# Part of a load goes over 15 DMA engines, so that the sixteenth carries 8 KB less

## The chip, the cores and the metric

One core of a Trainium2 chip. The metric is the device time of one execution in microseconds (us). The kernel before takes 120.12 us (median of three runs, 120.01 to 120.28).

## The reference

```python
x, y: (1024, 4096) float32
z = x * y
out = 0.5 * z * (1 + tanh(sqrt(2 / pi) * (z + 0.044715 * z ** 3)))
```

## The kernel before

Each of 128 partitions owns eight rows, 32,768 contiguous elements (128 KB) of x, y and the output. SP issues all transfers. x stays in SBUF whole, y goes through a ring of half that size; DVE multiplies in place, ACT applies the activation in place, and two stores take the halves out.

```python
X_LOADS = [(0, 16384), (16384, 32768)]
Y_LOADS = [(0, 16384, 0), (16384, 24576, 0), (24576, 31488, 8192), (31488, 32768, 15104)]
STORES  = [(0, 16384), (16384, 32768)]
...
def load_x(i):
    a, b = X_LOADS[i]
    return nc.sync.dma_start(out=xs[:, a:b], in_=x_r[:, a:b]).then_inc(sem_x[i], 16)
...
_hoist(nc, [load_x(0).ins, load_y(0).ins])        # issued first of all
load_x(1)
for i in range(1, len(Y_LOADS)):
    nc.sync.wait_ge(sem_mul, -(-(Y_LOADS[i][1] - Y_RING) // STEP))   # ring space is free
    load_y(i)
... # DVE waits for sem_x >= 16 and sem_y >= 16, multiplies; ACT follows
for i, (a, b) in enumerate(STORES):
    if i == 0:
        nc.sync.wait_ge(sem_y[-2], 16)            # no store before the third y load has landed
    nc.sync.wait_ge(sem_act, done[b])
    nc.sync.dma_start(out=out_r[:, a:b], in_=xs[:, a:b]).then_inc(sem_o[i], 16)
```

The queue of each DMA engine is thus: x first half, y first half, x second half, three pieces of y, two stores. The packet records of the trace before agree: eight packets an engine for each (65,536 bytes three times, then 32,768, 27,648, 5,120, and 65,536 twice), with an increment of 4 bytes after every eight.

Of the kernel before, what the change touches and what calls it, by code (L numbers as in the profile page):

```python
# [1 line left out]

# [4 lines left out]


F32 = mybir.dt.float32
GELU = mybir.ActivationFunctionType.Gelu_apprx_tanh  # L10


X_LOADS = [(0, 16384), (16384, 32768)]

Y_LOADS = [
    (0, 16384, 0),
    (16384, 24576, 0),
    (24576, 31488, 8192),
    (31488, 32768, 15104),
]  # L20
STEP = 4096
STORES = [(0, 16384), (16384, 32768)]
Y_RING = 16384


def _hoist(nc, issued):

    here = nc.cur_bb.bb.instructions
    first = nc.main_func.blocks[0].instructions
    for ins in issued:  # L30
        del here[next(k for k, i in enumerate(here) if i is ins or i.name == ins.name)]
    engine = issued[0].engine
    at = next(
        k
        for k, i in enumerate(first)
        if i.engine == engine and type(i).__name__ == "InstDrain"
    )
    first[at:at] = issued


@with_exitstack
def kernel(
    ctx: ExitStack,
    tc: tile.TileContext,
    x: bass.AP,
    y: bass.AP,
    out: bass.AP,
):
    nc = tc.nc
    P = nc.NUM_PARTITIONS  # L50

    x_r = x.flatten_outer_dims().rearrange("(p a) c -> p (a c)", p=P)
    y_r = y.flatten_outer_dims().rearrange("(p a) c -> p (a c)", p=P)
    out_r = out.flatten_outer_dims().rearrange("(p a) c -> p (a c)", p=P)
    total_f = x_r.shape[1]


    tc.close()
    tc.compile()  # L59

    xs = nc.alloc_sbuf_tensor("xs", [P, total_f], F32).ap()
    ys = nc.alloc_sbuf_tensor("ys", [P, Y_RING], F32).ap()
    sem_x = [nc.alloc_semaphore(f"sem_x{i}") for i in range(len(X_LOADS))]
    sem_y = [nc.alloc_semaphore(f"sem_y{i}") for i in range(len(Y_LOADS))]
    sem_mul = nc.alloc_semaphore("sem_mul")
    sem_act = nc.alloc_semaphore("sem_act")
    sem_o = [nc.alloc_semaphore(f"sem_o{i}") for i in range(len(STORES))]

    def load_x(i):
        a, b = X_LOADS[i]  # L70
        return nc.sync.dma_start(out=xs[:, a:b], in_=x_r[:, a:b]).then_inc(sem_x[i], 16)  # L71

    def load_y(i):
        a, b, r = Y_LOADS[i]
        return nc.sync.dma_start(
            out=ys[:, r : r + b - a], in_=y_r[:, a:b]
        ).then_inc(sem_y[i], 16)

    _hoist(nc, [load_x(0).ins, load_y(0).ins])
    load_x(1)  # L80
    for i in range(1, len(Y_LOADS)):
        nc.sync.wait_ge(sem_mul, -(-(Y_LOADS[i][1] - Y_RING) // STEP))
        load_y(i)

    n = 0
    done = {}
    for i, (a, b, r) in enumerate(Y_LOADS):
        for j, (xa, xb) in enumerate(X_LOADS):
            if xa <= a < xb:
                nc.vector.wait_ge(sem_x[j], 16)  # L90
        nc.vector.wait_ge(sem_y[i], 16)  # L91
        for c in range(a, b, STEP):
            w = min(STEP, b - c)
            nc.vector.tensor_mul(  # L94
                out=xs[:, c : c + w],
                in0=xs[:, c : c + w],
                in1=ys[:, r + c - a : r + c - a + w],
            ).then_inc(sem_mul, 1)
            n += 1
            done[c + w] = n  # L100
            nc.scalar.wait_ge(sem_mul, n)
            nc.scalar.activation(  # L102
                out=xs[:, c : c + w], in_=xs[:, c : c + w], func=GELU
            ).then_inc(sem_act, 1)

    for i, (a, b) in enumerate(STORES):
        if i == 0:
            nc.sync.wait_ge(sem_y[-2], 16)
        nc.sync.wait_ge(sem_act, done[b])
        nc.sync.dma_start(out=out_r[:, a:b], in_=xs[:, a:b]).then_inc(sem_o[i], 16)  # L110
    for i in range(len(STORES) - 1):
        nc.sync.wait_ge(sem_o[i], 16)
    nums = sorted(s.num for s in [*sem_x, *sem_y, *sem_o[:-1], sem_mul, sem_act])
    assert nums == list(range(nums[0], nums[-1] + 1))
    nc.sync.sem_clear(range(nums[0], nums[-1] + 1))
    nc.sync.wait_ge(sem_o[-1], 16).then_inc(sem_o[-1], -16)


# [1 line left out]
_INS = ['x', 'y']  # L120
_OUTS = [((1024, 4096), 'float32')]


# [23 lines left out]
```

## Time and profile before

| | before |
|---|---|
| time, median of 3 | 120.12 us |
| span of the trace | 118.7 us |
| DVE busy / ACT busy | 34.9 / 30.2 us |
| share of 16 DMA engines' time that packets fill | 98.6% |
| last landing of second x load / second y load / third y load / last store | 60.43 / 70.14 / 78.52 / 118.69 us |

The page is read from its DMA rows: compute is under a third busy, the DMA engines are full nearly everywhere. The landings are the times at which the trace sees each engine's increment of a transfer's semaphore. The lines themselves stand in the prediction.

### The profile page before, as it was taken

To read this page: it belongs to the slowest core of one execution; us is meant where nothing else is said; L and a number is where in the kernel's file an instruction comes from. 1 tells how busy PE (TensorE), PEld (TensorE's weight loads), DVE (VectorE), ACT (ScalarE), POOL (GpSimd) and SP (SyncE) were. 2 spreads that over 40 slices of the span, in tenths; PEclk is the share of its full clock that TensorE was granted. 3 is DMA by queue.
4 is the path that set the end of the run, shared out by engine and by line. 5 is a ranking of instruction groups with operands and counts; after the bars stand their busy time and mean duration, and the time that the engine had idled before them with its cause. 6 is when DMAs were issued, how large, how long until landed. Compare 5 with 4: busy or idle time off the path is not lost.

```text
span 118.7 us, 73 instructions
## 1 busy us (share of the span) xinstructions
DVE 34.9 (29%) x9; ACT 30.2 (25%) x10; POOL 0.2 (0%) x4
## 2 busy tenths in 40 slices
DVE  0000000000000199999700039999950000000000
ACT  3000000000000006797790000878995000000000
POOL 0000000000000000000000000000000000000000
DMA  9899888998899888988898989998889888988895
GB/s 353 353 420 640 353 353 353 662 397 353 353 552 508 353 353 375 684 353 353 353 497 386 453 375 447 447 574 353 353 353 707 353 353 353 707 353 353 353 486 221
DMA packets 1152, 50.33 MB, mean 424 GB/s; under 512 B 128, under 2 KB 128, under 8 KB 256
## 3 DMA queue, kind: packets, MB, share of 16 engines
q1 hardware_dynamic: 1152, 50.33, 98.6%
HBM read 33.55 MB, written 16.78 MB: 424 GB/s over the span
## 4 chain that ended last, share of the span: by engine, by line
DMA 51%; DVE 18%; ACT 6%; issue 0%; SPq 0%; DVEq 0%
DMA ys<-in_y_dram 51%; DVE xs L94 18%; ACT xs L102 6%; SPq L71 0%; DVEq L91 0%
## 5 line engine op out<-in xcount | busy, mean ns | idle before, releaser
L94 DVE TENSOR_TENSOR xs<-xs,ys 128x4096 f32<-128x4096 f32 (+2 forms) x9 | 34.9, 3946 | 52.8 <-DMA ys<-in_y_dram 52.8
L102 ACT ACTIVATE xs<-xs 128x4096 f32<-128x4096 f32 (+2 forms) x9 | 28.9, 3235 | 58.5 <-DVE xs L94 58.5
L102 ACT ACT_TABLE_LOAD x1 | 1.3, 1283 | 1.9 <-PEq L59 1.9
L131 POOL MEMSET const-bfloat16-1.0<- 128x1 bf16 x1 | 0.1, 102 | 0.0
L131 POOL MEMSET const-uint8-127<- 128x1 uint8 x1 | 0.1, 102 | 0.0
L131 POOL MEMSET const-float32-0.0<- 128x1 f32 x1 | 0.1, 99 | 0.2 <-issue 0.2
L131 POOL MEMSET const-float32-1.0<- 128x1 f32 x1 | 0.1, 99 | 0.0
## 6 DMA issues: line engine op xcount, KB each, us to landing
ys<-in_y_dram SPq DMA_DIRECT2D x1, 4096.0 KB, 20.2
ys<-in_y_dram SPq DMA_DIRECT2D x1, 3456.0 KB, 19.9
ys<-in_y_dram SPq DMA_DIRECT2D x1, 640.0 KB, 21.0
xs<-in_x_dram SPq DMA_DIRECT2D x2, 40.1
out_dram<-xs SPq DMA_DIRECT2D x2, 24.5
ys<-in_y_dram SPq DMA_DIRECT2D x1, 40.6
```

Source lines behind the costliest of these rows:

```text
L94: nc.vector.tensor_mul(out=xs[:, c : c + w], in0=xs[:, c : c + w], in1=ys[:, r + c - a : r + c - a + w],).then_inc(sem_mul, 1)
L102: nc.scalar.activation(out=xs[:, c : c + w], in_=xs[:, c : c + w], func=GELU).then_inc(sem_act, 1)
L131: nc = _bacc.Bacc("TRN2", target_bir_lowering=False, num_devices=1)
```

## The change

The intent is to take work off the DMA engine that is thought to end last. A transfer over 120 partitions is spread over 15 engines, and one over 8 partitions over 8; if 256 of the 16,384 columns go that way, one engine carries 8 rows of 1 KB less, and eight carry one more each. The trace before shows 16 landings for each of its transfers over 128 partitions and no other shape. The records don't number the engines: "the sixteenth" is the name of the one that carries less here, and "the first eight" are those with nine rows of 1 KB.

```diff
+RELIEF = 256
...
+    def load_x_15_engines(i):
+        a, b = X_LOADS[i]
+        for p, q, c, d in [(0, P, a + RELIEF, b), (0, 120, a, a + RELIEF), (120, P, a, a + RELIEF)]:
+            nc.sync.dma_start(out=xs[p:q, c:d], in_=x_r[p:q, c:d]).then_inc(sem_x[i], 16)
...
-    load_x(1)
+    load_x_15_engines(1)
...
-                nc.vector.wait_ge(sem_x[j], 16)
+                nc.vector.wait_ge(sem_x[j], 48 if j else 16)
```

## The prediction

> **What bounds the kernel now.** I read the page from its head: first the busy shares, then the slices of DMA share and GB/s, then the queue's total, the issues, the chain that ended last, the waits of the issuing engine (SP), and last the packet records of the trace around each transfer's end.
>
> ```profile
> span 118.7 us, 73 instructions
> DVE 34.9 (29%) x9; ACT 30.2 (25%) x10; POOL 0.2 (0%) x4
> ...
> DMA  9899888998899888988898989998889888988895
> ...
> q1 hardware_dynamic: 1152, 50.33, 98.6%
> HBM read 33.55 MB, written 16.78 MB: 424 GB/s over the span
> ```
>
> No compute engine is busy for a third of the span, and the one DMA queue's packets fill 98.6% of the time of 16 engines. Two thirds of the bytes are the loads of x and y, one third the stores. So this kernel is a copy with some arithmetic under it, and what can be won is only what lies around the packets: the start, the join between loads and stores, and the spread between the first and the last of the 16 engines at the end.
>
> ```profile
> DMA 51%; DVE 18%; ACT 6%; issue 0%; SPq 0%; DVEq 0%
> DMA ys<-in_y_dram 51%; DVE xs L94 18%; ACT xs L102 6%; SPq L71 0%; DVEq L91 0%
> ```
>
> The chain of waits is misleading in its tail: it goes over DVE and ACT and stops with ACT's last tile at 90.6 us, though the span lasts to 118.7. Nothing computes in those last 28 us; they are stores alone. The timeline puts the second store's issue right there (the group starts at 78.54 and ends at 90.95):
>
> ```profile
> 78.54 12.41 SPq L110 DMA_DIRECT2D out_dram<-xs  x2
> 79.03 3.62 ACT L102 ACTIVATE xs<-xs 128x4096 f32<-128x4096 f32 x1 [0.71 <-DVE xs L94]
> 83.36 7.22 ACT L102 ACTIVATE xs<-xs 128x4096 f32<-128x4096 f32 x3 [0.72 <-DVE xs L94]
> ```
>
> The first store's packets run until 99 us, so the second store, issued by 90.9, has 8 us of slack. The waits of SP say which wait could bind:
>
> ```profile
> SPq L110 <- DMA ys<-in_y_dram: 16.2, 1, 16.2
> ...
> SPq L115 <- DMA out_dram<-xs: 8.5, 1, 8.5
> ```
>
> The first line is the wait that holds the first store back until the third y load (27,648 bytes a partition) has landed on all of its engines. It ends at 78.52 us, and that is the one join where DMA engines go idle. The packet records show it: the last y load (5,120 bytes a partition) ends on the first engine at 79.08 us and on the last at 79.72, while the first store packets start at 79.38 on twelve or so engines within 0.1 us, and on the last two at 79.63 and 79.72. Early engines wait 0.3 us for the store, the two latest run from load to store without a gap. The sum of idle engine time there is 2.7 us, 0.17 us for each of 16.
>
> **The spread.** One packet is one partition's row, so each engine carries 8 packets of each transfer. The 16 end times of each transfer, relative to the first, are: second x load, 0 to 0.307 us for thirteen engines, then 0.41, 0.46 and 0.50; third y load, 0 to 0.27 for thirteen, then 0.385, 0.557 and 0.638; second store, 0 to 0.11 for fourteen, then 0.163 and 0.193. The first packets started over 0.60 us (1.00 to 1.60 us), so most of the spread is there from the first transfer on: it is a late start that is never made up, as all engines then move at one speed. Stalls add some in the third y load, where single packets of 1.04 to 1.12 us stand among the usual 1.025. The records don't name the engine. That the latest is the sixteenth is the change's own premise; the profile does not confirm or deny it.
>
> [...]128 partitions go over 16, 120 over 15 (8 rows each), 8 over 8 (one row each): just what the change wants. [...]The trace of before shows 16 landings for each of its 8 transfers and has no other shape, so it is silent on 120 and 8. [...]65,536 bytes in 2.420 us is 27.1 GB/s an engine. [...]In before, small rows of a queued transfer cost little: 5,120 bytes took 0.196 us, 26.1 GB/s.
>
> **The change part by part.** Packet times by size in the trace (medians) are 0.196, 1.025, 1.213 and 2.420 us for 5,120, 27,648, 32,768 and 65,536 bytes. A straight line through the first two: 0.829 us over 22,528 bytes, 0.0368 ns per byte, and 7.6 ns for each packet; it gives 1.213 and 2.419 for the other two. The semaphore packets (4 bytes) took 9 ns. With this line, for each engine:
>
> - Main piece, 8 rows of 64,512 bytes for 65,536: 8 x 1,024 x 0.0368 ns = 0.301 us less, on all 16.
> - 120-partition piece, engines 1 to 15: 8 rows of 1,024 bytes at 7.6 + 37.7 = 45 ns, 0.362 us, and one increment of 9 ns: 0.371 more.
> - 8-partition piece, engines 1 to 8: one row and one increment, 0.054 more.
>
> Sums: engines 1 to 8 get 0.124 us more (0.301 taken, 0.371 and 0.054 given), engines 9 to 15 get 0.070 more, the sixteenth 0.301 less. The total of the 16 grows by 8 x 0.124 + 7 x 0.070 - 0.301 = 1.18 us, or 0.07 us an engine, where all packets together are 116.3 us an engine (40 x 2.420 + 8 x 1.213 + 8 x 1.025 + 8 x 0.196 + 8 x 0.009).
>
> The issue side is free: two more issues on SP at about 0.33 us each (the rows of the loads in the timeline are 0.33 to 0.44) come at 2 to 3.3 us, and the engines reach the second x load at 40 us. The DVE's wait for 48 is free too: it needs the second x load with the second y load, and that lands ten microseconds later (70.14 us against 60.4).
>
> What then sets the end? If the sixteenth is the latest, it comes 0.301 us forward, and the one 0.02 to 0.08 us behind it takes over. At the third y load: latest 0.638, second 0.557 + 0.070 to 0.124 = 0.627 to 0.681, so the store's release moves by -0.01 to +0.04 us. At the end: second latest 0.163 + 0.070 to 0.124 = 0.233 to 0.287, against 0.193 before: 0.04 to 0.09 us later. The early engines' idle 0.3 us before the first store would absorb their own extra. My middle for the pure arithmetic is thus +0.05 us, with a possible gain near 0.1 us only if two engines that are late now are not late in most runs and the sixteenth alone is.
>
> **The rivals.** First, the sixteenth is the lone straggler in the usual run and this profile's second one is chance. Then the end moves from 0.193 to the bulk's 0.11 + 0.07 to 0.12, no gain at the end, but the store's release moves from 0.638 to about 0.48, and with it the thirteen engines that wait for it: 0.1 us gained, about 120.0 us. For it: the size of the relief (0.30 us) fits a gap of 0.25 to 0.37 between the latest and the thirteen. Against it: in every one of the 8 landings the two or three latest stand together. Second, the small rows cost more than the line says: [...]8 KB an engine takes twice as long. That adds up to 0.30 us on fifteen engines, and nothing gives it back: about 120.4 us. [...]against it: it is 8 KB of the 3,072 KB that an engine moves, and [...]engines that are 0.3 us apart may slip past each other. Third, nothing to see: the latest engine is not the sixteenth, everything shifts by 0.07 to 0.12 us, about 120.2 us, inside the spread of runs (120.01 to 120.28).
>
> **Range and chances.** Weights: pure arithmetic or nothing to see 0.5 (120.12 + 0.05 to 0.10), lone straggler 0.2 (120.0), port conflicts 0.3 (120.3 to 120.5). The mean is about 120.2 us. The runs of before differ by 0.27 us, so the range is 119.9 to 120.5. A change of 2% is 2.4 us, eight times the largest single term here, and would need DMA engines that stop for microseconds at the small transfers; 98.5% within, 1% slower, 0.5% faster.
>
> **What would show each step.** The packet count should be 1,152 + 128 + 23 = 1,303 and 50.33 MB as before; under 2 KB there should be 128 rows and 151 increments. The small rows should take about 45 ns each: 80 to 100 ns would speak for port conflicts. The landings of the second x load's parts should be 16, 15 and 8; the engine that has no 1 KB rows is the sixteenth, and its place in the order of end times before that point shows if it was the latest. The spread at the third y load should shrink from 0.64 to 0.5 or less only under the lone straggler. The prediction is wrong if the second x load's parts leave gaps of over 0.5 us on the engines, if the first store is released more than 0.2 us earlier, or if the time moves by over 0.4 us.

That the second rival's rows take twice as long was an assumption; experiment 2 later measured 5 KB rows at mostly 0.33 to 0.39 us in place of 0.196, while most 1 KB rows of the changed kernel took 46 ns. That 120 partitions go over 15 engines and 8 over 8 was also assumed. That engines 0.3 us apart may slip past each other is a guess, and no run shows it. "Port" is the word for a place where two engines meet; no record shows one, here or in the expectations below.

## The result, and the profile after

The changed kernel takes 120.53 us (median of 4, 120.37 to 120.79) against 120.15 (120.01 to 120.28) in the same rounds. The ratio is 1.0035, with a 95% interval of 1.0012 to 1.0057. A ratio here is the mean time of one kernel's runs over that of the other's of the same rounds, so it is not quite the ratio of the medians. The change is within 2%, as forecast, but it is a loss that is clear of noise, and the median lies 0.03 us above the range of 119.9 to 120.5.

The page of the changed kernel, in the rows that were shown of before:

```profile
span 119.3 us, 75 instructions
DVE 34.9 (29%) x9; ACT 30.2 (25%) x10; POOL 0.2 (0%) x4
...
DMA  9899988998899879977899899998889888988895
...
DMA packets 1303, 50.33 MB, mean 422 GB/s; under 512 B 151, under 2 KB 279, under 8 KB 407
...
q1 hardware_dynamic: 1303, 50.33, 98.7%
HBM read 33.55 MB, written 16.78 MB: 422 GB/s over the span
```

The bytes and the compute are the same, and the packets are the 1,303 that were counted beforehand. The span is 0.6 us longer, and yet the engines' time is as full as before (98.7% against 98.6%): the added time is not idle, packets take longer. That is the first thing to see here. The share of busy DMA time didn't tell moving from standing: a 32 KB packet that took 1.54 us in place of 1.21 (below) counts as busy throughout. The rate fell from 424 to 422 GB/s.

The waits of SP and the timeline's last rows:

```profile
SPq L117 <- DMA ys<-in_y_dram: 16.5, 1, 16.5
SPq L117 <- ACT xs L109: 11.9, 1, 11.9
SPq L122 <- DMA out_dram<-xs: 8.4, 1, 8.4
```

```profile
79.07 12.59 SPq L117 DMA_DIRECT2D out_dram<-xs  x2
79.74 3.62 ACT L109 ACTIVATE xs<-xs 128x4096 f32<-128x4096 f32 x1 [0.72 <-DVE xs L101]
84.07 7.22 ACT L109 ACTIVATE xs<-xs 128x4096 f32<-128x4096 f32 x3 [0.72 <-DVE xs L101]
```

The first store is issued at 79.07 us in place of 78.54. Everything after the second y load is the same chain as before, 0.5 to 0.7 us later. So the place to look is ahead of it, and the packet records of the trace have it. The second y load's rows are 32 KB. For one engine of the first eight, one that has no 8-partition row, and the sixteenth (the one whose large piece is followed by the second y load at once), the records of the two first traces read so (bytes, then ns of each packet; the engines of before have no names, all 16 are alike):

```
before, any engine       65536: 2427 to 2444  4: 9                            32768: 1213 to 1220
after, an early one      64512: 2380  4: 9  8 x 1024: 46  4: 9  1024: 46  4: 9  32768: 1520  1213 ...
after, no extra row      64512: 2394  4: 9  8 x 1024: 46  4: 9                  32768: 1525  1213 ...
after, the sixteenth     64512: 2380  4: 9                                      32768: 1536  1221 ...
```

Most small rows took 46 ns (109 of 128 at most 48 ns, 15 of them 60 to 118 ns, all from 59.9 us on), what the line through before's packets gave. Then one packet of 1.21 us took 1.42 to 1.59 us, on all 16 engines, and also on the one that had no small rows and was to be relieved.

To compare traces I sum, for each packet, its time over the line of the prediction (7.6 ns and 0.0368 ns per byte; 9 ns for an increment), from 37 to 62.5 us, and divide by 16. This is called the **stall** below. It is 0.02 us an engine in the first trace of before and 0.36 in the changed kernel's. A second figure is free of that line: the mean landing of the first y load to the mean landing of the second, a stretch in which each engine moves the second half of x and a quarter of y. This is called the **stretch**; it is 29.06 us before and 29.56 after. The first load's landing also moves from run to run (its last landing was at 21.75 us before, 21.97 after), which the stretch leaves out.

### The profile page after: what moved, and what is told of

It is laid out like the page before. It is cut to its first block, busy times and chain, and to the rows that moved or that the text cites. A ratio compares the mean times of both kernels' runs of the same rounds, so it can differ in the third digit from the quotient of the medians.

```text
span 119.3 us, 75 instructions
## 1 busy us (share of the span) xinstructions
DVE 34.9 (29%) x9; ACT 30.2 (25%) x10; POOL 0.2 (0%) x4
## 2 busy tenths in 40 slices
DMA packets 1303, 50.33 MB, mean 422 GB/s; under 512 B 151, under 2 KB 279, under 8 KB 407
## 3 DMA queue, kind: packets, MB, share of 16 engines
q1 hardware_dynamic: 1303, 50.33, 98.7%
## 4 chain that ended last, share of the span: by engine, by line
DMA 52%; DVE 18%; ACT 6%; issue 1%; SPq 0%; DVEq 0%
DMA ys<-in_y_dram 52%; DVE xs L101 18%; ACT xs L109 6%; SPq L73 0%; DVEq L98 0%
## 5 line engine op out<-in xcount | busy, mean ns | idle before, releaser
L109 ACT ACTIVATE xs<-xs 128x4096 f32<-128x4096 f32 (+2 forms) x9 | 28.9, 3234 | 59.2 <-DVE xs L101 59.2
```

The source lines that it names most:

```text
L109: nc.scalar.activation(out=xs[:, c : c + w], in_=xs[:, c : c + w], func=GELU).then_inc(sem_act, 1)
```

## The experiments

These are guesses to be tested. Theory P, "ports": a transfer cut over 120 and 8 partitions makes engines get in each other's way, so that its rows go at half speed and hold up the packet behind them. Theory D: 1 KB rows as such hold up the packet behind them. Theory H: 1 KB rows cost more when they all lie at one offset of a 128 KB row of the source. A "wrong on purpose" kernel loads other elements of x into 256 columns, with the same bytes and shapes.

### 1. The same cut over 128 partitions

```diff
-        for p, q, c, d in [(0, P, a + RELIEF, b), (0, 120, a, a + RELIEF), (120, P, a, a + RELIEF)]:
+        for p, q, c, d in [(0, P, a + RELIEF, b), (0, P, a, a + RELIEF)]:
-                nc.vector.wait_ge(sem_x[j], 48 if j else 16)
+                nc.vector.wait_ge(sem_x[j], 32 if j else 16)
```

> The same cut of the second x load (63 KB rows, then 1 KB rows), but the 1 KB rows in one transfer of 128 partitions over all 16 engines; nobody is relieved. In the changed kernel the first 32 KB packet after the small rows took about 1.54 us in place of 1.22 on 13 engines, 1.42 on the other three, also on the engine that had no small rows. Theory P[...]: the first 32 KB packets are back at 1.22 us, and the time is that of before plus 0.07 us. Theory H[...] and theory D[...]: the packets still take 1.5 us or so, and the time is 0.3 to 0.45 us over before.

Measured: 120.32 us against 120.13, ratio 1.0025 (1.0001 to 1.0048), runs from 120.15 to 121.1. In its trace all 16 first packets of 32 KB took 1,213 ns and all 1 KB rows 46 to 48; the stall is 0.01 us, the stretch 29.14. A window over the small rows, from 59.2 to 60.6 us, shows it in the profile. First the changed kernel, then this one; the columns are the window, its length, busy time on DVE, ACT and POOL, clock, DMA share and GB/s:

```profile
59.20:60.60 1.40, 0.00 (x0) 1.40 (x1) 0.00 (x0) 1.00 1.39 468
```

```profile
59.20:60.60 1.40, 0.00 (x0) 1.40 (x1) 0.00 (x0) 1.00 1.14 468
```

The share counts a packet's whole time where the packet starts, so it can pass 1 (1.39 and 1.14 here). The packets that start here carry the same bytes in both, and take 0.25 x 1.40 = 0.35 us an engine more in the changed kernel. That speaks for P and against D and H as the source of this stall. The times, though, scatter, and the trace is of one of the quick runs (120.20); later runs return to them.

### 2. 1,280 columns in place of 256, over 120 and 8 partitions and over 128

```diff
-RELIEF = 256
+RELIEF = 1280
```

> The change with 1,280 columns in place of 256: the rows of the 120- and the 8-partition transfers are 5 KB. Arithmetic alone: engines 1 to 8 get 5 KB more (0.196 + 0.009 us) and 0.07 us, the sixteenth 1.5 us less. Theory P: [...]1.5 us more on the fifteen, time 1.5 us or more over before. Theories H and D: 5 KB rows last 0.2 us each, the stall of the first 32 KB packet shrinks to under 0.1 us, and the time is 0.2 to 0.35 us over before.

Measured: 122.06 us against 120.13, ratio 1.0157 (1.0140 to 1.0174). Of its 128 rows of 5 KB, 21 took the 0.196 us of before, all of them among the first rows of their engine; 72 took 0.33 to 0.39. The first 32 KB packet took 1.80 to 2.18 us on fifteen engines, and on the sixteenth two packets took 1.95 and 2.64 in place of 1.21 each. The stall is 1.96 us an engine, the stretch 31.13.

The counterpart is the same size over 128 partitions (the diff of experiment 1 with RELIEF = 1280):

> The counterpart of the run with 1,280 columns: the same 5 KB rows, but in one transfer of 128 partitions[...]. Theory P: the 1.9 us of that run are gone, rows at 0.196 us and first 32 KB packets at 1.21, time 0.05 to 0.2 us over before. Theory D (small rows as such cost): a time well over 0.5 us above before.

Measured: 120.12 us against 120.19, ratio 0.9996 (0.9984 to 1.0008); stall 0.14 us (of which 0.12 before 57 us), stretch 29.25. The DMA view of both from 58.0 to 61.3 us, first with 120 and 8 partitions, then with 128:

```profile
DMA packets 180, 1.15 MB, mean 348 GB/s; under 512 B 37, under 2 KB 37, under 8 KB 165
## 3 DMA queue, kind: packets, MB, share of 16 engines
q1 hardware_dynamic: 180, 1.15, 139.1%
```

```profile
DMA packets 188, 1.57 MB, mean 477 GB/s; under 512 B 32, under 2 KB 32, under 8 KB 160
## 3 DMA queue, kind: packets, MB, share of 16 engines
q1 hardware_dynamic: 188, 1.57, 112.9%
```

The same loads, in rows of the same size, differ by 1.94 us in the median. What differs is that the small columns go in two transfers, over 120 and 8 partitions, in place of one over 128 (39 increments of 4 bytes for the second x load in place of 32). This pair is the clearest. The size fits in the main: 40 KB an engine at half speed would be 40,960 x 0.0368 ns = 1.51 us more (an estimate with the line through before's packets). The other 0.45 us of the stall is not explained. The 8-partition piece may have a part in it; no run leaves that piece out.

### 3. Other places in the HBM

Against experiment 1 (the line inside the loop goes too):

```diff
-        for p, q, c, d in [(0, P, a + RELIEF, b), (0, P, a, a + RELIEF)]:
+        nc.sync.dma_start(out=xs[:, a + RELIEF:b], in_=x_r[:, a + RELIEF:b]).then_inc(sem_x[i], 16)
+        skew = bass.AP(x_r.tensor, 0, [[total_f + RELIEF, P], [1, RELIEF]])
+        nc.sync.dma_start(out=xs[:, a:a + RELIEF], in_=skew).then_inc(sem_x[i], 16)
```

> As the split over 128 partitions, but the 1 KB rows are read from places that step by 1 KB more in each partition, so that no two lie at the same offset of a 128 KB row. The result is wrong on purpose in 256 columns of each partition. Theory H: the first 32 KB packets are back at 1.22 us, time 0.05 to 0.15 us over before. Theory D: still about 1.5 us, and time 0.3 to 0.45 us over before. Theory P: 1.22 us here and in the split over 128 alike.

Measured (128 partitions): 120.19 us against 120.13, ratio 1.0003 (0.9989 to 1.0017); first packets all 1,213 ns, stall 0.01 us, stretch 29.14. The trace is that of experiment 1. Theory D is out: small rows of the same size cost nothing that can be measured here.

### 4. The small pieces first

```diff
-        ... [(0, P, a + RELIEF, b), (0, 120, a, a + RELIEF), (120, P, a, a + RELIEF)]:
+        ... [(0, 120, a, a + RELIEF), (120, P, a, a + RELIEF), (0, P, a + RELIEF, b)]:
```

> The changed kernel with the two small transfers ahead of the large piece of the second x load. Theories P, H and D: the stall moves to the first 63 KB packet (2.70 us in place of 2.38), and the time stays that of the changed kernel, 0.3 to 0.45 us over before. A theory that the second y load's own descriptors come late (it is issued at 50 us, apart from the rest) has no stall here, and a time of 0.05 to 0.15 us over before.

Measured: 120.55 us against 120.13, ratio 1.0033 (1.0017 to 1.0048). The expected 2.70 us for the first 63 KB packet was missed: it took 2.47 to 2.53 on all 16 engines in place of 2.38; on the sixteenth, 2.53. The stall is 0.15 us, the stretch 29.25, yet the time is as long as the changed kernel's. So the second y load's own issue isn't the cause. A second look:

> The order with the small pieces first once more. Its first trace had a stall of only 0.09 to 0.15 us at the first 63 KB packet, yet its five times were 0.2 to 0.6 us over before. If the order makes the stall small, it is 0.1 us again; if the stall depends on how the engines happen to be staggered in a run, it is anything from 0.1 to 0.35 us.

Measured: 120.56 us (one run), first 63 KB packets 2.38 to 2.53, some 1 KB rows 0.14 to 0.36 us; stall 0.19, stretch 29.30. The smaller stall stayed. The two figures leave a part out in this order, though. The small rows now stand right behind the first y load, and its landing, where the stretch begins, is itself late: it comes 19.43 and 19.44 us after the first x load's (means of 16), and 19.34 us, within 0.01, in every other trace. From the first x load's landing to the second y load's it is 48.68 and 48.75 us here, 48.73 to 48.97 in the changed kernel's traces and 48.48 in the split's. So 0.1 us of what seemed missing lies ahead of the stretch. In the first trace, one engine also landed last at the end, 0.34 us after the mean of the 16 (0.12 in before).

### 5. Before and after once more, for the spread between traces

> The kernel before once more, for a second trace: how much of the difference between the two first traces is the start? In the first trace the first x load landed at 21.27 to 21.75 us and the second load of the queue at 40.63 to 41.08. If the start varies from run to run, the last landing of the first load lies between 21.7 and 22.0 us here; if the changed kernel starts later because of its two more issues, it is at 21.75 again.

Measured: 120.32 us (one run), first load landed last at 21.75 us, stall 0.05, stretch 29.19. This trace has a stall of its own, mostly past the window of that figure: from 62.5 to 81 us its packets took 0.43 us an engine over the line, against 0.09 in the first trace. 41 of its 128 packets of 32 KB took 1.24 to 1.29 us. All its transfers have 128 partitions. So a stall of this size can come without the change; what goes with the change is its place, at the small rows, in every trace.

> The changed kernel once more: if the stall at the first 32 KB packet belongs to the change, all 16 engines show 0.2 to 0.35 us over 1.213 again, on the engine without small rows too. The span is 118.9 to 119.4 us.

Measured: 120.31 us (one run), first 32 KB packets 1.26 to 1.46 us, the sixteenth's 1.37; stall 0.19, stretch 29.39. The same window as in experiment 1 has a share between the two lines there:

```profile
59.20:60.60 1.40, 0.00 (x0) 1.40 (x1) 0.00 (x0) 1.00 1.25 468
```

The stall at this place came back, with another size (that it varies with how the engines are staggered is a guess); two traces that differ by 0.3 us in span can't be compared without repeats.

### 6. Two halves of 64 partitions

```diff
-        ... [(0, P, a + RELIEF, b), (0, 120, a, a + RELIEF), (120, P, a, a + RELIEF)]:
+        ... [(0, P, a + RELIEF, b), (0, 64, a, a + RELIEF), (64, P, a, a + RELIEF)]:
```

> The small columns go in two transfers of 64 partitions[...]. Theory P: [...]the rows or the first 32 KB packet show 0.3 us an engine, and the time is 0.35 to 0.5 us over before. A theory that the stall comes from engines left out of a transfer (15 or 8 in place of 16): no stall, time 0.1 to 0.2 us over before.

Measured: 120.58 us against 120.13, ratio 1.0022 (1.0007 to 1.0037), seven runs from 120.17 to 121.38. In the trace first packets of 1.38 to 1.51 us on 15 engines, stall 0.37 us, stretch 29.58; 1 KB rows of 245 to 389 ns stand among the others, and at the second y load one engine landed 0.76 us after the next. The trace is of the slowest of the seven runs (121.38), and that engine explains most of it, as the first store waits for the last one. The stall is that of the changed kernel, and about what was expected under theory P (0.3). That two transfers of 64 partitions fall under theory P, and that no engine is left out of them, were assumptions; how many engines carried each half is not noted. If none was left out, the number of engines is not what matters. The times alone do not separate this kernel from experiment 1.

### 7. The changed kernel and the split on one chip

> The changed kernel again, on one chip and beside the same runs of before as the split over 128: theory P has it 0.2 to 0.45 us over before and 0.15 to 0.3 over the split over 128.

Measured: 120.52 us against 120.19, ratio 1.0029 (1.0017 to 1.0041); stall 0.44, stretch 29.63.

> The split of 256 columns over 128 partitions again, since its first times were scattered (120.15 to 121.1): theory P has it 0.05 to 0.2 us over before. If it is as slow as the changed kernel, then the extra packets and issues cost what the trace put down to the ports.

Measured: 120.33 us, ratio 1.0021 (1.0004 to 1.0039), runs from 119.99 to 120.81; stall 0.01, stretch 29.14. The trace was taken of the 119.99 us run. In time the two differ by less than theory P asked for: the split is slower than before by more than its traces show.

### 8. A later issue

```diff
+    nc.sync.wait_ge(sem_x[0], 16)
     load_x(1)
```

> The kernel before, with the second x load issued only when the first has landed (21.7 us in place of 1.9; the engines need it at 40 us). In both traces of before the first load landed last at 21.75 us, in most kernels with more issues at 1.9 to 3.1 us at 21.9 to 22.0. If issues during the first packets delay the start, this is at 21.75 or earlier and 0 to 0.2 us faster than before; if that difference is chance, the time is that of before.

Measured (on the kernel before): 120.13 us against 120.19, ratio 0.9994 (0.9982 to 1.0007), first load landed last at 21.76 us. No gain, and the start of the changed kernel's traces (21.81 to 22.04 us) is not shown to come from its issues: the kernel of experiment 10, which issues nothing more at the start, was at 21.92.

### 9. Is the common offset a part of it?

The changed kernel with the same skew as in experiment 3 under its 120 and 8 partitions:

```diff
+            src = x_r[p:q, c:d] if c > a else bass.AP(
+                x_r.tensor, p * (total_f + RELIEF), [[total_f + RELIEF, q - p], [1, RELIEF]])
-            nc.sync.dma_start(out=xs[p:q, c:d], in_=x_r[p:q, c:d]).then_inc(sem_x[i], 16)
+            nc.sync.dma_start(out=xs[p:q, c:d], in_=src).then_inc(sem_x[i], 16)
```

> The changed kernel with its 120- and 8-partition rows read from skewed places (wrong on purpose in those 256 columns). Ports as the whole cause: stalls as in the changed kernel, 0.15 to 0.45 us an engine in the trace, time 0.3 to 0.45 us over before. Offset in the HBM as a part of the cause: the stall stays in part, and the time is 0.1 to 0.25 us over before.

Measured: 120.34 us against 120.10, ratio 1.0014 (0.9999 to 1.0030); stall 0.28, stretch 29.47. The skewed split over 128 again, and one more look at the plain split:

> The skewed split over 128 partitions again (wrong on purpose). If same offsets make the unskewed split scatter, this one is again within 0.1 us of before and its runs within 0.3 us of each other; if the scatter is chance, it may be at 0.2 us over before with runs 0.5 us or more apart.

Measured: 120.16 us, ratio 1.0001 (0.9987 to 1.0015), runs within 0.28 us of each other.

> One more trace of the split of 256 columns over 128 partitions. If it falls on a slow run (over 120.4 us), the place of the lost time is told by the packets: over 0.1 us an engine around 59 to 62 us under the offset theory, at the start or elsewhere otherwise. A quick run (under 120.3) tells nothing new.

Measured: 120.15 us, a quick run, stall 0.00: it tells nothing new. Then the changed kernel and its skewed version side by side:

> The changed kernel beside its skewed version: 0.3 to 0.45 us over before. If ports are all of it, the two agree within 0.1 us; if the offset is a part, this one is 0.15 to 0.25 us slower than the skewed one.

Measured: 120.39 us against 120.22, ratio 1.0023 (1.0008 to 1.0038); stall 0.22, stretch 29.42.

> The skewed version of the changed kernel again (wrong on purpose): 0.3 to 0.45 us over before if ports are all of it, 0.1 to 0.25 if the offset is a part. The stall in its trace is 0.15 to 0.45 us an engine either way.

Measured: 120.38 us, ratio 1.0013 (0.9998 to 1.0029); stall 0.34, stretch 29.55. The medians are equal, the means 0.11 us apart, and the trace of the skewed one stalls more. So the pair does not settle it: its medians are what was expected if theory P is all of it (though the changed kernel fell short of the 0.3 to 0.45 us expected of it), while both skewed calls lie where they were expected if the offset is a part (0.1 to 0.25 us over before). The means over all calls are these (before: 59 runs, 120.16):

| 256 columns | source at one offset | source skewed |
|---|---|---|
| 120 and 8 partitions | 120.50 (16 runs) | 120.36 (12 runs) |
| 128 partitions | 120.38 (13 runs) | 120.18 (11 runs) |

By time alone, then, the narrow transfers cost 0.11 us with the plain source and 0.18 with the skewed one, and the common offset costs 0.14 with narrow transfers and 0.21 with wide ones, so that neither is the whole loss of 0.34. The plain split is also the most scattered (119.99 to 121.1), and the 1,280-column split isn't slow (5 runs, 120.14); this would fit a cost of 1 KB rows at a common offset in some runs. No trace fell on a slow run of the split, so this is a suspicion and not shown.

### 10. The relief in the last store

```diff
-        nc.sync.dma_start(out=out_r[:, a:b], in_=xs[:, a:b]).then_inc(sem_o[i], 16)
+        pieces = [(0, P, a, b)] if i == 0 else [
+            (0, P, a + 256, b), (0, 120, a, a + 256), (120, P, a, a + 256)]
+        for p, q, c, d in pieces:
+            nc.sync.dma_start(out=out_r[p:q, c:d], in_=xs[p:q, c:d]).then_inc(sem_o[i], 16)
...
-    nc.sync.wait_ge(sem_o[-1], 16).then_inc(sem_o[-1], -16)
+    nc.sync.wait_ge(sem_o[-1], 48).then_inc(sem_o[-1], -48)
```

> The kernel before with the relief in the last store in place of the second x load: large piece first, then the 120- and the 8-partition pieces, and nothing behind them. If ports are shared on the way out as on the way in, the last engines end 0.3 to 0.4 us later, and so does the kernel; if only the engines count, fifteen engines end 0.07 to 0.12 us later and the time is 0 to 0.1 us over before.

Measured: 120.66 us against 120.10, ratio 1.0036 (1.0020 to 1.0053). From 82 us to the end the packets' excess is 0.31 us an engine, against 0.06 in before. So the relief costs about as much on the way out, where nothing follows it, as on the way in. The place is another: here the packet ahead of the small rows is long. The last 63 KB row of each engine took 2.39 to 2.76 us in place of 2.38, and the 1 KB rows 46 ns for the most part, up to 181. The same cut of the store over 128 partitions was not run, so here the cost isn't tied to the cut over 120 and 8.

No version that was run beats the kernel before; the later issue and the 1,280-column split over 128 are at its time.

### All traces on one scale

| kernel | traces | stall, us an engine | stretch, us |
|---|---|---|---|
| before | 2 | 0.02, 0.05 | 29.06, 29.19 |
| before, later issue | 1 | 0.02 | 29.07 |
| before, relief in the last store | 1 | 0.07 | 29.11 |
| changed | 4 | 0.36, 0.19, 0.44, 0.22 | 29.56, 29.39, 29.63, 29.42 |
| changed, skewed source | 2 | 0.28, 0.34 | 29.47, 29.55 |
| small pieces first (see experiment 4) | 2 | 0.15, 0.19 | 29.25, 29.30 |
| two halves of 64 partitions | 1 | 0.37 | 29.58 |
| changed with 1,280 columns | 1 | 1.96 | 31.13 |
| split over 128, 256 columns | 3 | 0.01, 0.01, 0.00 | 29.14, 29.14, 29.14 |
| split over 128, skewed source | 2 | 0.01, 0.01 | 29.14, 29.14 |
| split over 128, 1,280 columns | 1 | 0.14 | 29.25 |

From 37 to 62.5 us the relief in the last store changes nothing, so the first three rows show how far traces differ by chance here. The four traced runs of the changed kernel took 120.62, 120.31, 120.72 and 120.30 us: the time follows the stall.

## Why the prediction was wrong

**What bounds the kernel, the issue side, the waits.** Right. DMA time sets the end; the wait for 48 and the two more issues (1.20 us for the three, from 1.92 us on) cost nothing that shows; the packet counts are exact (1,303, of them 128 rows of 1 KB and 151 increments). The second x load's semaphore shows the 39 landings that were expected (16, 15 and 8), and two records at 2.90 and 3.29 us, before any of its data. DVE, which waits for 48 there, went on at 70.94 us; that those two records brought the missing nine is an inference.

**The sum of the small rows.** Right as far as it went. A 1 KB row took 46 ns against 45 worked out, and in the split over 128 partitions, which pays the same 8 rows and one increment, the stretch is 29.14 us against 29.06 and 29.19 in the two traces of before.

**The step that failed is the choice among the rivals.** The middle took the small rows at the cost of the line, 0.07 to 0.12 us an engine, and nothing for what they do to the packets around them. The second rival was written down with its size, up to 0.30 us on fifteen engines. It was weighted at 0.3 and left out of the middle, with the argument, a guess, that engines 0.3 us apart might slip past each other. The four traces of the changed kernel show stalls of 0.36, 0.19, 0.44 and 0.22 us an engine, 0.30 in the mean, and the split over 128 at most 0.01: the stall of transfers that are cut over 120 and 8 partitions was the missing term. The rival's own total was also short: it gave about 120.4, without the 0.07 to 0.12 us of the small rows on top of the 0.30. Together they are 0.37 to 0.42 us on 120.15, that is 120.52 to 120.57; measured were 120.53 in the first rounds, and 120.50 in the mean of 16 runs over all calls, where 59 runs of before have 120.16. That the sum meets the time so closely is in part luck: by time alone the narrow transfers account for only 0.11 to 0.18 of the 0.34 us (experiment 9).

**The premise and the relief.** The sixteenth engine, the one with no small rows, can be made out in most of these traces where its large rows end: it is the latest by 0.10 and 0.11 us in two, and among the latest three, within 0.15 us of the last, in most others. So it is late, but not alone, as the landings of before suggested. (The prediction's gap of 0.25 to 0.37 us between the latest engine and the thirteen is 0.37 at the third and last y loads by packet ends, but 0.09 to 0.20 at the six other transfers; for a lone straggler it was read too favourably.) More important, relief did not relieve it. It skipped 0.30 us of rows and then lost 0.16 to 0.32 us on its next packet where that could be read on the changed kernel (1,371 and 1,536 ns for 1,213); with 1,280 columns it skipped 1.5 us and lost 2.2. Why the engine without small rows is held up with the others is not shown; experiments 1 and 2 show only that this goes with the cut over 120 and 8 partitions.

**What would have shown it.** The prediction said that its second rival, "port conflicts", would show as 1 KB rows of 80 to 100 ns. They took 46 ns for the most part; the stall came out in the packet behind, with 1,280 columns half in the rows (1.0 us an engine) and half behind them (0.9), and in the store in the packet ahead. So here a stall was booked on a neighbour of the packets that bring it. The spread at the third y load, predicted at 0.63 to 0.68 us without a lone straggler, was 0.72 by packet ends in the first trace and 0.53 in the second, so one trace could not have told.

**Open.** Whether 1 KB rows at one offset cost part of the changed kernel's 0.34 us: the plain split's times (1.0025, 1.0021) say that something besides the cut over 120 and 8 costs up to 0.2 us, its three traces, all of quick runs, show nothing. Also open is what stalled the second trace of before, and where in the chip the engines meet, if they do: the runs show that the cut over partitions brings the stall, not where it arises.

## What to carry to other kernels

Before taking work off one DMA engine, run the same cut over all 128 partitions beside it: 5 KB rows of transfers over 120 and 8 partitions took mostly 0.33 to 0.39 us in place of 0.196, part of the time was paid by the packets around them, and the engine that was relieved was held up too (1.54 us for a packet of 1.21). In a kernel like this, whose queue is full, keep transfers at 128 partitions; if columns must be cut, cut them over all 128 (rows of 5 KB then cost nothing, ratio 0.9996; rows of 1 KB may cost 0.2 us). When the expected gain is a fraction of a microsecond, a listed rival of the same size belongs into the sum, not beside it.
